# The second chunk's attention outputs summed three products behind the gate, with the decode columns formed apart

## The chip, the cores and the metric

The kernel runs on one core of one Trainium2 chip. The core has a matrix engine (TensorE, PE in the profile, with its weight loads as PEld), three engines for elementwise work (VectorE, DVE; ScalarE, ACT; GpSimd, POOL) and a queue engine (SyncE, SP) that issues most of the DMA transfers; GpSimd issues the others. The metric is device time in microseconds, and a time is the median of the runs. TensorE's granted clock is given as a share of full speed.

## The reference

The kernel computes one inference step of a two-layer decoder of width 2048, with 1024 prompt tokens and 8 decode tokens. Layer A is a pooling mixer. Layer B, where the change lies, is sliding-window attention over keys and values shared from layer A's output, with 32 query heads of 64, a learned sink per head and a gate:

```python
def attn_layer(x, pos, kb, vb, k_pos, q_pos, blocked, w_in, sinks, w_out, g_ln, b_ln):
    z = x @ w_in                                   # 2048 -> queries (2048) and gate (2048)
    q = rope_partial(z[..., :D_ATTN].reshape(B, T, N_HEADS, HEAD_DIM), pos)
    gate = z[..., D_ATTN:]
    ...
    o = attn_core(q, kb, vb, q_pos, k_pos, sinks).reshape(B, T, D_ATTN)
    y = (o * jax.nn.silu(gate)) @ w_out            # 2048 -> 2048
    return layer_norm(ALPHA * x + y, g_ln, b_ln)
```

`o * silu(gate)` is what this text calls the attention outputs. The prompt tokens go through it blocked by the window of 128, the 8 decode tokens against a cache of keys and values.

## The kernel before

Tokens are columns. Chunk 0 holds prompt tokens 0 to 511, chunk 1 the tokens 512 to 1023 and, as its last 8 columns, the decode tokens (520 columns). Features lie on the 128 partitions in 16 tiles. The phases run one after another: `ai`, `ao` (layer A, in and out), `bi` (layer B's keys, values, queries and gate, with the attention mixed in) and `bo` (output projection), each for chunk 0 and chunk 1; in the profile's order of time they end with bi of chunk 0, bi of chunk 1 (called bi1, first product at 1542.9 us), bo of chunk 0 (bo0, from 1990.3) and bo of chunk 1 (bo1, from 2172.8).

**Products.** Most matrix work goes through Strassen's scheme: a block of two by two quarters takes seven products in place of eight. One product is 24 matmuls (`seven`, L641 to L643): eight contraction tiles, each as weight-high by input-high, weight-high by input-low and weight-low by input-high. High is a rounded cast on ScalarE (L474 for weights, L752 for inputs), low the rest, subtracted on VectorE (L489 and L761). The lines L582 to L614 move the products' results out of the accumulators on ScalarE and VectorE (L602 and L607 are VectorE's).

**Sums of inputs.** Four of the seven products of a block use sums of quarters of the input: E and O are two neighbouring feature tiles, a and b the two halves of their columns. `t_ops` (L809 to L812) forms the four sums on VectorE in a fresh slot, GpSimd's queue stores them to a tensor in DRAM (L813; `to` for the attention outputs), and the slot is freed at once. When the phase that needs them comes near, `x_load` reads them back (L742).

**Slots.** Nearly everything lives in 53 slots of 128x1040 floats (`Mem`; `m` in the profile). A request takes the whole slot that has been free for longest, or a half one. A slot that is freed with a store still in flight is marked ten releases younger, so that others go first if there are others. A write to a slot waits for the store that still reads it.

**The order.** Every engine executes the program in its written order (`in_order`). That order is set by counting products: `at(n, f)` puts work n products ahead, after that product's matmuls; `product(n, rank, f)` does so for matmuls. `begin` fetches the weights ahead: up to 7 products loaded, 4 cast and 3 complete, less in bi1 when under four whole slots are free (`ahead`). Side work (`side`, `extra`) advances by a step between products as slots allow: the sums of output weights (`sum_gen`, L422 to L428, tensor `swob`) in bi1, and `t_gen` in bo0.

**Attention.** `attend` spreads one pair of heads (tile t) over about 14 products: scores (L1742), the copy and the mask (L1759, L1763), exponentials (L1778), normalization (L1791), transposes (L1795), copies of the transposed weights (L1804, L1805), value products (L1819), and last `gate`: VectorE multiplies the outputs by the gate (L1828) into half a slot, and GpSimd stores the 512 prompt columns (L1831). In chunk 0 `gate` also runs `t_ops` at every second tile. In chunk 1 it doesn't, since the decode tokens' outputs come from elsewhere (`decode`, whose last step `s9` stores eight tiles by eight columns from `sgd` to the same DRAM tensor, L1966); there both are joined in DRAM, and in bo0, from product 18, `t_gen` reads the pairs of tiles back (L822) and runs `t_ops` on them, one pair every second product.

The scores need the rotated queries: `q_done` and `rope` (L1607, L1714) run on VectorE in program order with everything else there.

Of the kernel before, what the change touches and what calls it, by code (L numbers as in the profile page):

```python
# [9 lines left out]
F32 = mybir.dt.float32  # L10
# [6 lines left out]
P = 128  # L17
D = 2048
NK = D // P
SEQ = 1024  # L20
NDEC = 8
# [3 lines left out]
NH = 32  # L25
# [5 lines left out]
TP = 512  # L31
# [39 lines left out]
)  # L71

LATE = (2, 3)
X_KEEP = 5
X_AGE = 3
SIDE_KEEP = 5
# [105 lines left out]
class Kern:  # L182
    def __init__(self, ctx, tc, io):
        self.tc, self.io = tc, io
        self.nc = tc.nc
        pool = lambda name, **kw: ctx.enter_context(tc.tile_pool(name=name, **kw))
        one = pool("one", bufs=1)
        self.smp = pool("smp", bufs=2)
        dram = pool("dram", bufs=1, space=bass.MemoryType.DRAM)
        self.psd = [pool(f"psd{i}", bufs=1, space=bass.MemoryType.PSUM) for i in range(3)]  # L190
        self.pso = pool("pso", bufs=1, space=bass.MemoryType.PSUM)
        self.four = None
        ctx.callback(self.use_four, None)
        self.prm = one.tile([P, N_PRM], F32, name="prm")
        self.cst = one.tile([P, N_CST], F32, name="cst")
        self.mki = one.tile([P, P], I32, name="mki")
        self.jr = one.tile([P, P], F32R, name="jr")
        self.nsink = one.tile([P, NH], F32, name="nsink")
        self.carry = one.tile([P, NK, NST], F32, name="carry")
        self.kdec = one.tile([P, 2, NDEC], F32, name="kdec")  # L200
        self.qd = [one.tile([P, NDEC, 8], F32, name=f"qd{i}") for i in range(2)]
        self.sgd = [one.tile([P, 8, NDEC], F32, name=f"sgd{i}") for i in range(2)]
        self.mem = Mem(pool("mem", bufs=1), NSLOT)
        self.n = 0
        self.i = self.e = self.lastO = self.turns = self.ring = 0
        self.posts, self.events, self.side = [], {}, []
        self.extra, self.on = None, False
        self.fresh = False
        self.ahead = 7, 4, 3
        dr = lambda n, s: dram.tile(s, F32, tag=n, name=n)  # L210
        self.Td, self.act, self.l_sq, self.l_sh = {}, {}, {}, {}
        for c, (_, T) in enumerate(CHUNKS):
            for n, k in (("x", "ai"), ("g", "ao"), ("h", "bi"), ("o", "bo")):
                if (k, c) in STRASSEN:
                    self.Td[n, c] = dr(f"t{n}{c}", [P, 8, 4, T // 2])
            self.act["x", c] = io[f"x{c}"]
            for n in ("g", "h", "o", "p"):
                self.act[n, c] = dr(f"{n}{c}", [P, NK, T])
        self.gbd = dram.tile([32, 2 * P], F32, tag="gbd", name="gbd")
        self.ws = {  # L220
            n: [dr(f"s{n}{q}", [P, 4, 1024]) for q in range(np_)]
            for n, np_ in (("wia", 16), ("woa", 8), ("wkv", 2), ("wib", 16), ("wob", 8))
        }
# [230 lines left out]
    def sums(self, name, q):  # L454

        self.hurry = name
        while self.summed.get(name, 16) <= q:
            if name != "wob":
                self.side_step()
            elif next(self.extra, 1):  # L460
                self.extra = None
        self.hurry = None
# [263 lines left out]
    def x_load(self):  # L726
        i, g = k = self.xl.pop(0)
        key = self.xkey
        T = CHUNKS[key[1]][1]
        TH = T // 2  # L730
        s = self.mem.full()
        if self.xseven:
            t = s.v(4, TH)
            if i in (0, 4, 5):
                k0, h = {0: (0, 0), 4: (1, 1), 5: (1, 0)}[i]
                src = self.act[key][:, 8 * g + k0 : 8 * g + 8 : 2, h * TH : (h + 1) * TH]
            else:
                src = self.Td[key][:, 4 * g : 4 * g + 4, {1: 0, 2: 1, 3: 2, 6: 3}[i], :]
        else:
            t = s.v(2, T)  # L740
            src = self.act[key][:, 4 * g + i : 4 * g + 4 : 2, :]
        self.nc.sync.dma_start(t, src)  # L742
        self.xraw[k] = s, self.i

    def x_cast(self, k):
        if k not in self.xraw:
            assert k == self.xl[0]
            self.x_load()
        s, _ = self.xraw.pop(k)
        n = 4 * (CHUNKS[self.xkey[1]][1] // 2) if self.xseven else 2 * TP  # L750
        h = self.mem.full()
        self.nc.scalar.copy(h.r[:, :n], s.a[:, :n])  # L752
        self.xhi[k] = s, h, n, self.i

# [536 lines left out]
    def phase_end(self, c, xs, x_in, pre, acc, gc, bc, out):  # L1291
# [14 lines left out]
        X, Y, gx, box = {}, {}, {}, {}  # L1306
        io = self.io
        A2 = slice(0, 2 * P)
        four = self.small(NK * 4, 1)
        f3 = four[:].rearrange("p (k t) -> p k t", k=NK)  # L1310
        b2 = lambda x: x[:, None, :].to_broadcast([P, 2, TH])

        def less(p):
# [414 lines left out]
    def attend(self, c, t, at, s1, s2, late=False):  # L1728
# [96 lines left out]
        def gate():  # L1825
            a = self.ao[c, t] = self.mem.half()
            z, j = self.sg.pop((c, t))
            nc.vector.scalar_tensor_tensor(  # L1828
                a.a[:, :TP], x["o"][:, :TP], 0.5, z.a[:, j * T : j * T + TP], op0=ALU.mult, op1=ALU.mult
            )  # L1830
            nc.gpsimd.dma_start(self.act["o", c][:, t, :TP], a.a[:, :TP])  # L1831
            if c == 1:
                self.ao.pop((c, t)).free(True)
            elif t % 2:
                e = self.ao.pop((c, t - 1))
                self.t_ops(e.a[:, :TP], a.a[:, :TP], self.Td["o", c], t // 2, T // 2)
                e.free(True)
                self.ao.pop((c, t)).free(True)
            if j == 1 or t == 15 or self.sg.get((c, t + 1), (None,))[0] is not z:
                z.free()  # L1840

# [6 lines left out]
        self.at(at + s1 + 1, keep)  # L1848
        self.product(at + s1 + s2, 1, values)
        self.at(at + s1 + s2 + 1, gate)  # L1850

    def gate_done(self, c, t0, s, n):
        nc = self.nc
# [28 lines left out]
    def decode(self, c, pr):  # L1882
# [77 lines left out]
        def s9():  # L1960
            a3 = self.sgd[pr][:]
            nc.vector.scalar_tensor_tensor(
                a3, x["p"][:, :64].rearrange("p (b t) -> p t b", t=8), 0.5, a3,
                op0=ALU.mult, op1=ALU.mult,
            )
            nc.sync.dma_start(self.act["o", c][:, 8 * pr : 8 * pr + 8, TP:], a3)  # L1966
            x["v"].free()
            W.free()

# [111 lines left out]
    def run(self):  # L2081
# [10 lines left out]
        def add(key, gen):  # L2092
            self.needs.append((key, gen))
            self.side.append(gen)

        acc, before = {}, False
        for n, (kind, c, part) in enumerate(PHASES):
# [20 lines left out]
            if n == 0:  # L2118
                pass
            elif (kind, c) == ("ai", 0):  # L2120
                add(("x", 1, False), self.t_gen(("x", 1)))
                self.room = 99
            elif (kind, c) == ("ai", 1):
                add(("g", 0, False), self.t_gen(("g", 0)))
                self.summed["woa"] = 0
                add("woa", self.sum_gen("woa"))
                self.every = 1.7
            elif (kind, c) == ("ao", 0):
                self.every = 2
            elif (kind, c) == ("ao", 1):  # L2130
                gen = self.ln_gen(0, *acc[0], C_GA, C_BA, self.act["h", 0], None)
                self.at(3, lambda gen=gen: add(("h", 0, True), gen))
                self.every = 2
            elif (kind, c) == ("bi", 0) and not self.strassen:
                self.summed["wob"] = 0
                self.extra = self.sum_gen("wob")
                for k in (4, 24):
                    self.at(k, lambda k=k: setattr(self, "on", k == 4))
                add(("h", 1, False), self.ln_gen(1, *acc[1], C_GA, C_BA, self.act["h", 1], self.Td.get(("h", 1))))
                add(("h", 0, False), self.t_gen(("h", 0)))  # L2140

                for k in range(10):
                    self.at(2 * k + 3, lambda: self.side and self.lastO < self.i - 1 and self.side_step())
                self.every = 1.2
            elif (kind, c) == ("bi", 1):
                self.at(8, lambda: setattr(self, "on", True))
                self.every, self.room = 1, 0
            elif (kind, c) == ("bo", 0):
                self.at(23, lambda: setattr(self, "ahead", (7, 4, 3)))
                self.at(18, lambda: add(("o", 1, False), self.t_gen(("o", 1))))  # L2150
                self.at(16, lambda: [s.free() for s in self.kv])
                self.rt.free()
            elif (kind, c) == ("bo", 1):
                gen = self.ln_gen(0, *acc[0], C_GB, C_BB, io["y0"], None)
                self.at(3, lambda gen=gen: add("y", gen))
                self.every = 3
# [154 lines left out]
```

## Time and profile before

| | |
|---|---|
| time before, median of 3 runs (lowest to highest) | 2367.22 us (2366.88 to 2370.61) |
| profiled execution, its own time | 2367.62 us |
| span from the first to the last instruction | 2365.9 us |
| TensorE busy | 2326.4 us, 98% |
| VectorE busy | 1923.5 us, 81% |
| ScalarE busy | 1342.2 us, 57% |
| GpSimd busy | 201.5 us, 9% |
| mean granted TensorE clock | 0.996 |

A busy share is the time in which an engine executes something, over the span. "Idle before, <- releaser" tells which instruction ended the time in which an engine stood idle; a DMA as a releaser is named by what it writes and reads, as in `to<-m`. Tiles are named without their numbers: `m` is any slot, `pD`, `pS` and `pO` are accumulators, `sm` small tiles. L numbers are lines of the kernel before; where the changed kernel's lines differ, the text says so.

### The profile page before, as it was taken

To read this page: it belongs to the slowest core of one execution; us is meant where nothing else is said; L and a number is where in the kernel's file an instruction comes from. 1 tells how busy PE (TensorE), PEld (TensorE's weight loads), DVE (VectorE), ACT (ScalarE), POOL (GpSimd) and SP (SyncE) were. 2 spreads that over 40 slices of the span, in tenths; PEclk is the share of its full clock that TensorE was granted. 3 is DMA by queue.
4 is the path that set the end of the run, shared out by engine and by line. 5 is a ranking of instruction groups with operands and counts; after the bars stand their busy time and mean duration, and the time that the engine had idled before them with its cause. 6 is when DMAs were issued, how large, how long until landed. Compare 5 with 4: busy or idle time off the path is not lost. (4 is left out here: it accounts for less than half of the span.)

```text
span 2365.9 us, 46542 instructions
## 1 busy us (share of the span) xinstructions
PE 2326.4 (98%) x18424; PEld 2219.4 (94%) x18424; DVE 1923.5 (81%) x2385; ACT 1342.2 (57%) x2429; POOL 201.5 (9%) x379
## 2 busy tenths in 40 slices
PE   8999999999999999999999999999999999999997
PEld 6899999999999999998778899999999999999997
DVE  8787998776878878868888888887777768888887
ACT  4444446544536547554554656685666667546556
POOL 0111110001000000000111111100000000000000
PEclk9999999999999999999999999999999999999999
DMA  8678789889889989989888766788787768699785
GB/s 294 215 244 303 274 291 349 308 308 315 286 278 365 331 270 324 334 314 330 282 324 322 258 230 224 238 297 275 232 259 221 222 193 298 227 353 371 259 302 194
DMA packets 252059, 669.18 MB, mean 283 GB/s; under 512 B 25760, under 2 KB 106560, under 8 KB 251840
## 3 DMA queue, kind: packets, MB, share of 16 engines
q1 hardware_dynamic: 206368, 501.14, 64.0%
q0 software_dynamic: 45472, 165.07, 17.9%
q8 instruction: 144, 2.36, 0.4%
q14 instruction: 75, 0.61, 0.1%
HBM read 471.01 MB, written 185.59 MB: 278 GB/s over the span
## 5 line engine op out<-in xcount | busy, mean ns | idle before, releaser
L641 PE MATMUL pD<-m,m 128*128 128x260 f32 (+1 forms) x4752 | 1346.9, 283 | 9.9 <-DVE m L602 3.7
L643 PE MATMUL pD<-m,m 128*128 128x260 f32 (+1 forms) x4752 | 1340.5, 282 | 4.5 <-DVE m L489 4.5
L642 PE MATMUL pD<-m,m 128*128 128x260 f32 (+1 forms) x4752 | 1340.3, 282 | 0.0
L641 PEld LDWEIGHTS pD<-m,m 128*128 128x128 f32 x4752 | 896.0, 189 | 21.0 <-issue 10.2
L643 PEld LDWEIGHTS pD<-m,m 128*128 128x128 f32 x4752 | 896.7, 189 | 6.0 <-DVE m L489 6.0
L642 PEld LDWEIGHTS pD<-m,m 128*128 128x128 f32 x4752 | 896.3, 189 | 0.5
L489 DVE TENSOR_TENSOR m<-m,m 128x1024 fp32r<-128x1024 f32 x674 | 814.1, 1219 | 96.1 <-ACT m L474 58.3
L474 ACT CAST m<-m 128x1024 fp32r<-128x1024 f32 x674 | 701.6, 1048 | 305.2 <-DVE m L332 71.3
L669 PE MATMUL pD<-m,m 128*128 128x512 f32 x448 | 179.7, 401 | 8.0 <-ACT m L752 8.0
L670 PE MATMUL pD<-m,m 128*128 128x512 f32 x448 | 177.2, 396 | 0.5 <-DVE m L761 0.5
L671 PE MATMUL pD<-m,m 128*128 128x512 f32 x448 | 177.2, 396 | 0.0
L761 DVE TENSOR_TENSOR m<-m,m 128x1024 fp32r<-128x1024 f32 (+1 forms) x120 | 146.9, 1225 | 7.2 <-ACT m L752 5.7
L614 ACT COPY m<-pD 128x260 f32<-128x260 f32 (+1 forms) x83 | 31.0, 373 | 188.2 <-PE pD L643 188.1
L752 ACT CAST m<-m 128x1024 fp32r<-128x1024 f32 (+1 forms) x120 | 125.7, 1052 | 14.2 <-PE pD L670 5.2
L669 PEld LDWEIGHTS pD<-m,m 128*128 128x128 f32 x448 | 84.7, 189 | 29.9 <-ACT m L752 8.0
L332 DVE TENSOR_TENSOR m<-m,m 128x1024 f32<-128x1024 f32 x88 | 107.6, 1222 | 5.9 <-DMA m<-in_wia 4.2
L670 PEld LDWEIGHTS pD<-m,m 128*128 128x128 f32 x448 | 84.8, 189 | 20.4 <-DVE m L761 1.6
L671 PEld LDWEIGHTS pD<-m,m 128*128 128x128 f32 x448 | 84.6, 189 | 19.8
L602 DVE TENSOR_TENSOR m<-pD,m 128x260 f32<-128x260 f32 (+1 forms) x86 | 36.4, 424 | 81.9 <-PE pD L643 78.6
L1778 ACT ACTIVATE m<-m,sm 128x128 f32<-128x128 f32 x256 | 99.2, 390 | 0.0
L1071 PE MATMUL pD<-m,m 128*128 128x260 f32 (+1 forms) x528 | 91.5, 323 | 0.0
L607 DVE TENSOR_TENSOR m<-pD,m 128x260 f32<-128x260 f32 (+1 forms) x84 | 35.6, 424 | 64.2 <-PE pD L643 64.0
(243 smaller groups left out, 2167.3 us busy)
## 6 DMA issues: line engine op xcount, KB each, us to landing
m<-in_wia SPq DMA_DIRECT2D x124, 512.0 KB
m<-in_wib SPq DMA_DIRECT2D x120, 512.0 KB
swia<-m POOLq DMA_DIRECT2D x64, 512.0 KB, 4.9
m<-swia SPq DMA_DIRECT2D x64, 512.0 KB
m<-swoa SPq DMA_DIRECT2D x64, 512.0 KB
swib<-m POOLq DMA_DIRECT2D x64, 512.0 KB, 5.3
m<-swib SPq DMA_DIRECT2D x64, 512.0 KB
m<-swob SPq DMA_DIRECT2D x56, 512.0 KB
```

The lines of the kernel that those rows point to most:

```text
L332: self.nc.vector.tensor_add(s[out].a[:, :1024], s[x].a[:, :1024], s[y].a[:, :1024])
L474: self.nc.scalar.copy(hi.r[:, :1024], self.stream[self.cast].src().a[:, :1024])
L489: self.nc.vector.tensor_sub(lo.r[:, :1024], s.src().a[:, :1024], hi.a[:, :1024])
L641: nc.tensor.matmul(ps[:, :TH], wh[:, s], h, start=new and k == 0, stop=False, skip_group_check=on)
L642: nc.tensor.matmul(ps[:, :TH], wh[:, s], l, start=False, stop=False, skip_group_check=on)
L643: nc.tensor.matmul(ps[:, :TH], wl[:, s], h, start=False, stop=k == 7, skip_group_check=on)
L669: nc.tensor.matmul(ps[:], wh[:, s], h, start=par == 0 and k == 0, stop=False)
L670: nc.tensor.matmul(ps[:], wh[:, s], l, start=False, stop=False)
L671: nc.tensor.matmul(ps[:], wl[:, s], h, start=False, stop=par == 1 and k == 7)
L752: self.nc.scalar.copy(h.r[:, :n], s.a[:, :n])
L761: self.nc.vector.tensor_sub(l.r[:, :n], s.a[:, :n], h.a[:, :n])
L1778: nc.scalar.activation(x["s3"][:, i, :], x["s3"][:, i, :], AF.Exp, bias=nm[:, i : i + 1], scale=0.125, accum_out=rs[:, i : i + 1],)
```

## The change

- In chunk 1, `gate` sets the last 8 columns of its half slot to zero on GpSimd, and copies columns 252 to 259 of the tile (the 8 columns of the second half's prompt tokens that stand opposite to the decode tokens) to a small tile `oa`.
- At every second tile `gate` runs `t_ops` on the two half slots over all 520 columns, for chunk 1 not at once but three products later, and frees the two half slots then. For chunk 0 the sums stay where they were.
- `t_gen` for the attention outputs of chunk 1, with its eight loads of 520 KB, is gone from bo0.
- The sums' columns that involve decode tokens are formed apart: `o_dec`, called by `gate` and by `decode`, counts its calls for each half of the tiles; when the eight tiles and the decode result are there, four small VectorE operations on 4x8 columns write them to `otd`, one product later.
- When bo1's inputs are cast (`x_cast`), ScalarE first writes these columns from `otd` over the loaded sums (eight small copies).
- `phase_end` takes its small tile `four` from `oa` in place of a tile of its own.

```diff
+TROW = {1: 0, 2: 1, 3: 2, 6: 3}
...
+        self.oa = one.tile([P, NH // 2, NDEC], F32, name="oa")
+        self.otd = one.tile([P, NK // 2, 4, NDEC], F32, name="otd")
+        self.odn = {}
...
         h = self.mem.full()
+        if self.xkey == ("o", 1) and k[0] in TROW:
+            t = s.v(4, THM)[:, :, THM - NDEC : THM]
+            self.nc.scalar.copy(t, self.otd[:, 4 * k[1] : 4 * k[1] + 4, TROW[k[0]], :])
         self.nc.scalar.copy(h.r[:, :n], s.a[:, :n])
...
-        four = self.small(NK * 4, 1)
-        f3 = four[:].rearrange("p (k t) -> p k t", k=NK)
+        four = self.oa[:].rearrange("p k t -> p (k t)")[:, : NK * 4]
+        f3 = four.rearrange("p (k t) -> p k t", k=NK)
...
             nc.gpsimd.dma_start(self.act["o", c][:, t, :TP], a.a[:, :TP])
             if c == 1:
-                self.ao.pop((c, t)).free(True)
-            elif t % 2:
+                nc.gpsimd.memset(a.a[:, TP:T], 0.0)
+                nc.gpsimd.tensor_copy(self.oa[:, t, :], a.a[:, THM - NDEC : THM])
+                self.o_dec(t // 8)
+            if t % 2:
                 e = self.ao.pop((c, t - 1))
-                self.t_ops(e.a[:, :TP], a.a[:, :TP], self.Td["o", c], t // 2, T // 2)
-                e.free(True)
-                self.ao.pop((c, t)).free(True)
+
+                def sums():
+                    self.t_ops(e.a[:, :T], a.a[:, :T], self.Td["o", c], t // 2, T // 2)
+                    e.free(True)
+                    self.ao.pop((c, t)).free(True)
+
+                if c == 1:
+                    self.at(3, sums)
+                else:
+                    sums()
...
+    def o_dec(self, pr):
+
+        self.odn[pr] = self.odn.get(pr, 0) + 1
+        if self.odn[pr] < 9:
+            return
+
+        def go():
+            nc = self.nc
+            d, o = self.sgd[pr][:], self.oa[:, 8 * pr : 8 * pr + 8, :]
+            Ea, Oa, Eb, Ob = o[:, 0:8:2, :], o[:, 1:8:2, :], d[:, 0:8:2, :], d[:, 1:8:2, :]
+            t = self.otd[:, 4 * pr : 4 * pr + 4]
+            nc.vector.tensor_sub(t[:, :, 1, :], Ea, Eb)
+            nc.vector.tensor_sub(t[:, :, 2, :], Eb, Ob)
+            nc.vector.tensor_add(t[:, :, 0, :], Ob, t[:, :, 1, :])
+            nc.vector.tensor_sub(t[:, :, 3, :], Oa, t[:, :, 0, :])
+
+        self.at(1, go)
...
             nc.sync.dma_start(self.act["o", c][:, 8 * pr : 8 * pr + 8, TP:], a3)
+            self.o_dec(pr)
...
                 self.at(23, lambda: setattr(self, "ahead", (7, 4, 3)))
-                self.at(18, lambda: add(("o", 1, False), self.t_gen(("o", 1))))
                 self.at(16, lambda: [s.free() for s in self.kv])
```

More of the change, by code (lines that the diff above doesn't have):

```diff
@@ L737, in x_load @@
             else:
-                src = self.Td[key][:, 4 * g : 4 * g + 4, {1: 0, 2: 1, 3: 2, 6: 3}[i], :]
+                src = self.Td[key][:, 4 * g : 4 * g + 4, TROW[i], :]
         else:
```

## The prediction

> **What bounds the kernel now.** I read the page first, then the windows and TensorE's own waits by stage, then the time lines around the gates.
>
> ```profile
> PE 2326.4 (98%) x18424; PEld 2219.4 (94%) x18424; DVE 1923.5 (81%) x2385; ACT 1342.2 (57%) x2429; POOL 201.5 (9%) x379
> ```
> TensorE is busy for 98% of the span, so every microsecond by which it is made to wait comes on top, and work taken from another engine is worth only the waits of TensorE that it ends. The next two views show where those are: the windows of a part of the second chunk's query and gate phase (bi1; columns: PE, PEld, DVE, ACT and POOL busy us, granted clock, DMA share, GB/s) and of the stretch of the first chunk's output phase (bo0) that holds the sums today, then TensorE's waits in all of bo0.
>
> ```profile
> 1540.00:1740.00 200.00, 199.66 (x1751) 194.40 (x1751) 156.90 (x204) 132.54 (x287) 12.61 (x20) 1.00 0.80 264
> ...
> 2075.00:2150.00 75.00, 75.00 (x638) 75.00 (x637) 62.95 (x82) 35.79 (x48) 6.39 (x12) 1.00 1.00 359
> ```
> ```profile
> PE pD L643 <- DVE m L489: 3.5, 5, 1.4
> PE pD L641 <- DVE m L602: 1.0, 1, 1.0
> PE pS L1819 <- DVE m L1805: 0.7, 1, 0.7
> PE pD L641 <- ACT pD L582: 0.3, 1, 0.3
> PE pD L629 <- ACT m L614: 0.3, 1, 0.3
> ```
> In bi1 TensorE does not wait though VectorE is 78% busy (156.9 of 200): it runs ahead. In bo0 it waits 5.8 us in all, but none of that lies in 2075 to 2150, where TensorE is busy 75.00 of 75.00.
>
> **The sums that move.** Eight groups of four VectorE operations leave products 26 to 43 of bo0.
>
> ```profile
> L812 DVE TENSOR_TENSOR m<-m,m 128x260 f32<-128x260 f32 x8 | 3.4, 430 | 0.3
> L809 DVE TENSOR_TENSOR m<-m 128x260 f32<-128x260 f32 x8 | 3.4, 424 | 0.0
> ```
> ```profile
> L813 POOL DMA_DIRECT2D to<-m x8: 531/531/533, 2087.5 to 2132.8; - x8
> ```
> The four are alike, 3.4 us for eight, so 13.6 us; they and their stores run from 2085 to 2133, inside the stretch without a wait. The eight loads of 520 KB on SyncE's queue that go with them fed only these sums. Removing all of it is worth 0; the upper bound is the 5.8 us of bo0 (a rival below). The changed program's instruction order places the groups at products 51, 65, 79, 93, 107 and 120 of bi1, and 6 and 19 of bo0: two stay in bo0. In bi1 a group costs VectorE 1.5 us (start to start of its operations) in place of a part of the output weights' sums, which the order shifts later because fewer slots are free, still inside bi1. VectorE's idle 22% covers it: 0, and 1.5 us each if it did not.
>
> **The stores that go with them.** A group's tile is freed as soon as its store is issued. In the changed program only two to five whole slots are free in bi1, and the next request for a slot takes this very one. Its writer must wait until the store has landed:
> ```
> L816..L819 to tile m43, L820 store m43 (DMASW7); next L493 VectorE m43   [waits DMASW7]   product 51
>                    L820 store m20 (DMASW3); next L277 SyncE load m20  [waits DMASW3]   product 65
>                    L820 store m28 (DMASW0); next L478 ScalarE m28     [waits DMASW0]   product 79
>                    L820 store m40 (DMASW6); next L478 ScalarE m40     [waits DMASW6]   product 93
>                    L820 store m40 (DMASW4); next L493 VectorE m40     [waits DMASW4]   product 107
> ```
> (L820, L478 and L493 are L813, L474 and L489 before.) The last three groups' slots are not asked for soon. What a landing takes, and that such a wait exists today, is in the groups of DMA issues (last column: median us to landing), in the answer for the tile `to`, and in ScalarE's waits in bo0:
>
> ```profile
> swob<-m POOLq DMA_DIRECT2D x32, 512.0 KB, 6.0
> ...
> to<-m POOLq DMA_DIRECT2D x8, 520.0 KB, 7.6
> ```
> ```profile
> DMA to landing us min/median/max: 2.9/6.7/9.3
> ```
> ```profile
> ACT m L474 <- DMA to<-m: 7.0, 4, 3.0
> ```
> So landing is between 2.9 and 9.3 us. I take 6.0, since the `swob` stores, of nearly this size, share bi1's lighter DMA load (0.80, against 1.00 where the 7.6 was). The issue starts 0.4 us after the sums (L812 ends near 2087.1, L813 starts at 2087.5), so a slot is blocked for 6.4 us. In bo0 ScalarE waited up to 3.0 us for it without harm; in bi1 the blocked engine has the chain to the next score matmuls behind it. The rows of product 51:
>
> ```profile
> 1716.07 1.23 DVE L489 TENSOR_TENSOR m<-m,m 128x1024 fp32r<-128x1024 f32 x1 [1.04 <-ACT m L1778]
> ...
> 1721.30 1.22 DVE L1805 TENSOR_TENSOR m<-pS,cst 128x1024 f32<-128x1024 f32 x1 [1.11 <-ACT m L1804]
> 1722.44 2.38 DVE L1607 TENSOR_TENSOR m<-m,m 128x1040 f32<-128x1040 f32 x2
> 1724.86 1.24 DVE L1714 TENSOR_TENSOR m<-m,m 128x1040 f32<-128x1040 f32 x1
> ```
> ```profile
> 1727.46 1.78 PE L1742 MATMUL pS<-m,m 64*128 64x256 f32 x14
> ```
> Product 51: the sums end at 1716.6, the store lands at 1723.0. VectorE then has L489, two small ones (0.4), L489, L1805, two L1607 and L1714 in a row: 7.5 us, to 1730.5. Queued behind the wait are thus the next weights' low parts and the rope of the queries; who waits is L1742, which started at 1727.46: **+3.1**. Product 65: a SyncE load some six loads ahead of its use waits: **0** (6.4 at worst, if that lead were gone).
>
> ```profile
> 1819.83 0.29 DVE L1940 TENSOR_SCALAR m<-m,sm 128x128 f32<-128x128 f32 x1
> ```
> ```profile
> 1822.32 1.04 ACT L474 CAST m<-m 128x1024 fp32r<-128x1024 f32 x1
> ...
> 1824.49 1.00 ACT L1804 COPY m<-pS 128x1024 f32<-128x1024 f32 x1
> ```
> ```profile
> 1831.04 2.00 PE L1742 MATMUL pS<-m,m 64*128 64x256 f32 x16
> ```
> Product 79: the sums follow L1940 and end at 1821.5, landing 1827.9. ScalarE is blocked, and behind it stand two casts, the eviction L591, a third cast and L1804 (4.3 us together); then L1805, a small copy, L1607 twice and L1714 on VectorE (5.1): 1837.3, against 1831.04: **+6.3** (of these some 4.1 already at the eviction).
>
> ```profile
> 1867.15 2.36 DVE L489 TENSOR_TENSOR m<-m,m 128x1024 fp32r<-128x1024 f32 x2 [0.26 <-issue]
> ...
> 1916.89 2.36 DVE L489 TENSOR_TENSOR m<-m,m 128x1024 fp32r<-128x1024 f32 x2
> ```
> ```profile
> 1882.36 2.00 PE L1742 MATMUL pS<-m,m 64*128 64x256 f32 x16
> ...
> 1932.48 2.00 PE L1742 MATMUL pS<-m,m 64*128 64x256 f32 x16
> ```
> Product 93: the sums take 1869.4 to 1870.9, landing 1877.3; with the chain of product 79 without the small copy 9.1 us, 1886.4 against 1882.36: **+4.0**. Product 107: 1919.2 to 1920.7, landing 1927.1, 7.5 us as at 51, 1934.6 against 1932.48: **+2.2**. Together **+15.6**. With a landing of L the four are L−2.9, L+0.3, L−2.0 and L−3.8, never below 0.
>
> [...]
>
> **The clock.** A long enough wait of TensorE costs again behind it:
>
> ```profile
> 360.74 0.39 PE L641 MATMUL pD<-m,m 128*128 128x256 f32 x1 [1.94 <-ACT pD L582]
> ```
> ```profile
> PE pD L641 <- ACT m L1778: 2.6, 1, 2.6
> ```
> ```profile
> 360.70:364.80 4.10, 4.06 (x21) 4.06 (x22) 4.07 (x4) 3.22 (x4) 0.53 (x1) 0.59 1.04 371
> 1364.00:1368.30 4.30, 4.30 (x24) 4.30 (x25) 4.26 (x5) 0.85 (x1) 1.06 (x2) 0.61 0.62 250
> ```
> ```profile
> PE pD L641 <- DVE m L602: 1.4, 1, 1.4
> ```
> After waits of 1.94 and 2.6 us the granted clock is 0.59 and 0.61 over some 4 us; after one of 1.4 us (at 2233) no such stretch is seen. In bi1 a matmul takes 199.66 / 1751 = 0.114 us, so the two stretches lost 4.06 − 21 × 0.114 = 1.7 and 4.30 − 24 × 0.114 = 1.6. Of the new waits those of product 79 (4.1) and 93 (2.2 at its eviction) are past 1.9: 2 × 1.6 = **+3.2**; bounds 0 and 4 × 1.6 = 6.4. [...]
>
> **bo0.** VectorE around product 19, where the eighth group and the decode columns' second four operations now stand (ahead of and behind L602):
>
> ```profile
> 2021.97 1.23 DVE L1805 TENSOR_TENSOR m<-pS,cst 128x1024 f32<-128x1024 f32 x1 [2.23 <-ACT m L1804]
> ...
> 2059.11 1.22 DVE L1263 TENSOR_TENSOR m<-m,m 128x1024 f32<-128x1024 f32 x1
> ...
> 2063.65 0.42 DVE L602 TENSOR_TENSOR m<-pD,m 128x256 f32<-128x256 f32 x1
> ...
> 2079.33 3.49 DVE L489 TENSOR_TENSOR m<-m,m 128x1024 fp32r<-128x1024 f32 x3
> ```
> ```profile
> 1822.19 0.17 DVE L1785 TENSOR_TENSOR sm<-sm,sm 128x8 f32<-128x8 f32 x1 [0.32 <-ACT m L1778]
> ```
> VectorE has no gap from 2059 to 2082.8, and TensorE's waits for L489 at products 20 and 22 lie here, so what is added is paid in full: 1.5 for the group, and for four operations on 4x8 columns four times between L1785's 0.17 (8 columns) and L1940's 0.29 above (128 columns), 0.7 to 1.2, 0.9 taken as 32 columns are nearer to the former: **+2.4**; 0 if TensorE's queue of weights were deeper there than the waits say. The seventh group, at product 6, falls ahead of the first row, into 2.23 us of VectorE's idleness: 0, at most 1.5. The first decode four stand in bi1: 0, at most 0.9.
>
> **GpSimd and ScalarE.**
> ```profile
> L1381 POOL COPY sm<-m 128x8 f32<-128x8 f32 x8 | 4.7, 605 | 32.7 <-DVE m L612 29.9 <-DVE m L1263 1.4 <-DMA m<-p 1.4
> ```
> ```profile
> L1864 ACT COPY sgd<-m 128x16 f32<-128x16 f32 x8 | 1.6, 201 | 0.0
> ```
> Sixteen copies of 128x8 at 0.6 us and as many memsets (smaller) are under 20 us of an engine that is 9% busy. They stand behind the store of the gate's output and ahead of later stores; the sums that need them come three products later: 0 (0.6 a gate at most). Eight ScalarE copies at 0.2: one lies ahead of an eviction (L614) that TensorE waits for, **+0.2**; at most 1.6. Taking `four` from another tile costs no instruction: 0.
>
> **Sum:** 15.6 + 3.2 + 2.4 + 0.2 = 21.4. The profiled execution took 2367.62, 0.4 over the median of 2367.22: 2389.0 against its own time, **2388.6** as a median.
>
> **Rivals.**
> - *B, the queues hide it.* Bi1's weights are prepared products ahead, and ScalarE's waits for the same stores in bo0 cost nothing. Then only bo0's 2.6 stays: 2369.8. Against it: L1714 ended at 1726.1, 1.3 us before L1742 at 1727.46, and that is all the lead the rope has.
> - *C, quick landing* at the observed 2.9: 0, 3.2, 0.9 and 0, no fall of the clock past 1.9 save one: 4.1 + 1.6 + 2.6 = 8.3, 2375.5.
> - *D, faster.* If VectorE's 13.6 us out of bo0 let its queue get ahead, TensorE's 5.8 us of waits there go: 2361.4. That decides only if B holds and the eighth group is covered. Against it: the waits lie at products 14 to 22 and 51 to 55, the removed work at 26 to 43, and what VectorE may prepare ahead is limited.
> - *E, late landing.* At the maximum of 9.3 (a POOL queue with a weight store ahead): 6.4 + 9.6 + 7.3 + 5.5 = 28.8, four falls 6.4, bo0 2.6: 37.8, 2405.
>
> **How the numbers follow.** The forecast 0.60 (its own range, landing 4 to 8: 2379 to 2399), B 0.15, C 0.10, D 0.07, E 0.08. A measurement here can tell about 0.2%, 4.7 us, from no change: B is "same", D "faster", the rest "slower" (0.78). The range 2369 to 2401 leaves out D, half of E and the forecast's ends.
>
> **What will show it.** Right: ScalarE's and VectorE's waits list casts (L478, L493) waiting for DMA `to<-m` of 3 to 6 us in bi1; TensorE waits for L1721 or L595 near 1728, 1830, 1885 and 1935, with granted clock under 1 behind two of them; bi1 longer by 15 to 20 us, bo0 by 2 to 3. Wrong: bi1 as long as before (447 us between its first products), or bo0 shorter by its waits. It would be wrong most of all if landings in bi1 differ from 6 us, as each microsecond counts four times.

## The result, and the profile after

The changed kernel takes 2394.49 us (median of 5 runs, 2391.82 to 2396.11) against 2368.41 before (now five runs, the three of above among them): a ratio of 1.0111, 95% interval 1.0099 to 1.0122, so 26 us slower. The forecast was 2388.6 us, slower, in a range of 2369 to 2401. The profiled execution took 2394.49 us with a span of 2392.7, against 2367.62 and 2365.9: 26.8 more in the span. (In the changed kernel L813 is L820, L474 L478, L489 L493, L591 L595, L602 L606, L641 to L643 L645 to L647, L1714 L1721, L1742 L1749, L428 L432.)

From the first product of one phase to that of the next, bi1 takes 475.6 us in place of 447.4 (+28.2), bo0 182.3 in place of 182.5. So the cost is all in bi1. The windows of bi1, of the kernel before and of the changed one (columns: PE, PEld, DVE, ACT, POOL busy us, granted clock, DMA share, GB/s):

```profile
1543.00:1990.30 447.30, 446.45 (x3997) 433.14 (x3996) 330.37 (x431) 298.29 (x689) 23.88 (x38) 1.00 0.76 242
```
```profile
1541.50:2017.10 475.60, 455.44 (x3996) 440.92 (x3997) 339.10 (x458) 298.22 (x688) 31.18 (x70) 0.97 0.71 233
```
TensorE executes the same matmuls, but stands idle for 475.60 − 455.44 = 20.2 us in place of 0.85 (+19.3), and is busy for 9.0 us longer, at a granted clock of 0.97. Both parts are one cause. TensorE's waits in bi1, and the waits of VectorE and of ScalarE for stores of sums:

```profile
PE pD L645 <- ACT m L595: 19.2, 4, 8.0
PE pS L1749 <- DVE m L1721: 0.5, 2, 0.3
PE pD L645 <- ACT pD L586: 0.4, 1, 0.4
```
```profile
ACT m L478 <- DMA to<-m: 7.7, 1, 7.7
```
```profile
DVE m L493 <- DMA to<-m: 12.8, 2, 7.5
```
Four waits of TensorE make up 19.2 us, where before the whole phase had one of 0.85. How one comes about is seen on VectorE and then on ScalarE and TensorE behind the sums of product 51:

```profile
1723.08 1.23 DVE L493 TENSOR_TENSOR m<-m,m 128x1024 fp32r<-128x1024 f32 x1 [7.54 <-DMA to<-m]
```
```profile
1724.34 1.04 ACT L478 CAST m<-m 128x1024 fp32r<-128x1024 f32 x1 [8.70 <-DVE m L493]
1725.29 0.37 ACT L595 COPY m<-pD 128x260 f32<-128x260 f32 x1
```
```profile
1725.71 0.58 PE L645 MATMUL pD<-m,m 128*128 128x260 f32 x1 [4.17 <-ACT m L595]
```
VectorE's L493 writes the slot that the sums have just left, and waits 7.54 us for their store. ScalarE's next cast waits for this L493, the eviction L595 stands behind the cast in ScalarE's order, and TensorE's next product waits for the eviction. Where the cast is itself the one that waits for the store, at product 79, it stands 9.5 us; the landings of all these stores span nearly the same range as before (2.9/6.7/9.3 then):

```profile
1836.03 1.04 ACT L478 CAST m<-m 128x1024 fp32r<-128x1024 f32 x1 [9.49 <-issue]
```
```profile
DMA to landing us min/median/max: 2.9/6.0/9.0
```
(The profile names no releaser there; in the trace the store lands at 1835.96, just ahead of the cast, and the run hold79 below shows that it is the store.) TensorE's four waits are 4.17, 7.96, 5.21 and 1.82 us at products 53, 81, 95 and 109. At each the clock falls; the windows that begin shortly before their ends:

```profile
1725.00:1732.00 7.00, 6.29 (x36) 6.06 (x38) 5.46 (x5) 6.14 (x14) 0.00 (x0) 0.53 0.00 0
1839.00:1848.00 9.00, 8.23 (x68) 7.75 (x70) 7.41 (x10) 7.35 (x15) 0.00 (x0) 0.71 0.16 51
1898.00:1906.00 8.00, 7.21 (x61) 6.78 (x63) 6.55 (x7) 6.92 (x15) 0.00 (x0) 0.73 0.00 2
1952.00:1960.00 8.00, 7.00 (x60) 6.60 (x62) 6.45 (x7) 7.02 (x15) 0.00 (x0) 0.79 0.21 60
```
That DMA is nearly at rest in these windows (0.00 to 0.21, against 0.71 in all of bi1) would fit loads that wait, too, for slots that the stalled engines have yet to leave; no run was made on that.

In bo0 the sum of TensorE's waits is as before, but other ones make it up:

```profile
PE pD L647 <- DVE m L493: 2.9, 4, 1.4
PE pD L645 <- DVE m L606: 1.5, 1, 1.5
PE pD L633 <- ACT m L618: 0.8, 1, 0.8
PE pS L1826 <- DVE m L1812: 0.7, 1, 0.7
```
The wait for L606 at product 20, ahead of which the eighth group and the decode columns now stand, is new (1.5). At products 51 to 55, where 2.6 us were lost before, only 0.8 is left.

### The profile page after: what moved, and what is told of

Its sections match the earlier page's. It is cut to its first block, busy times and chain, and to the rows that moved or that the text cites. A ratio compares the mean times of both kernels' runs of the same rounds, so it can differ in the third digit from the quotient of the medians.

```text
span 2392.7 us, 46615 instructions
## 1 busy us (share of the span) xinstructions
PE 2333.9 (98%) x18424; PEld 2226.5 (93%) x18424; DVE 1925.4 (80%) x2393; ACT 1344.3 (56%) x2437; POOL 207.3 (9%) x411
## 5 line engine op out<-in xcount | busy, mean ns | idle before, releaser
L645 PE MATMUL pD<-m,m 128*128 128x260 f32 (+1 forms) x4752 | 1350.5, 284 | 28.8 <-ACT m L595 19.2
L647 PE MATMUL pD<-m,m 128*128 128x260 f32 (+1 forms) x4752 | 1342.8, 283 | 3.9 <-DVE m L493 3.9
L645 PEld LDWEIGHTS pD<-m,m 128*128 128x128 f32 x4752 | 899.0, 189 | 40.7 <-ACT m L595 20.0
L493 DVE TENSOR_TENSOR m<-m,m 128x1024 fp32r<-128x1024 f32 x674 | 814.6, 1220 | 122.3 <-ACT m L478 71.6
L647 PEld LDWEIGHTS pD<-m,m 128*128 128x128 f32 x4752 | 899.5, 189 | 5.1 <-DVE m L493 5.1
L646 PEld LDWEIGHTS pD<-m,m 128*128 128x128 f32 x4752 | 899.3, 189 | 0.5
L478 ACT CAST m<-m 128x1024 fp32r<-128x1024 f32 x674 | 701.1, 1048 | 329.1 <-DVE m L336 71.8
L673 PEld LDWEIGHTS pD<-m,m 128*128 128x128 f32 x448 | 84.9, 189 | 30.1 <-ACT m L759 8.1
L606 DVE TENSOR_TENSOR m<-pD,m 128x260 f32<-128x260 f32 (+1 forms) x86 | 36.5, 424 | 91.3 <-PE pD L647 91.1
L674 PEld LDWEIGHTS pD<-m,m 128*128 128x128 f32 x448 | 84.9, 190 | 19.9 <-DVE m L768 1.0
L675 PEld LDWEIGHTS pD<-m,m 128*128 128x128 f32 x448 | 84.7, 189 | 19.9
L1078 PEld LDWEIGHTS pD<-m,m 128*128 128x128 f32 x528 | 79.5, 188 | 8.2
```

The lines of the kernel that those rows point to most:

```text
L478: self.nc.scalar.copy(hi.r[:, :1024], self.stream[self.cast].src().a[:, :1024])
L493: self.nc.vector.tensor_sub(lo.r[:, :1024], s.src().a[:, :1024], hi.a[:, :1024])
L645: nc.tensor.matmul(ps[:, :TH], wh[:, s], h, start=new and k == 0, stop=False, skip_group_check=on)
L646: nc.tensor.matmul(ps[:, :TH], wh[:, s], l, start=False, stop=False, skip_group_check=on)
L647: nc.tensor.matmul(ps[:, :TH], wl[:, s], h, start=False, stop=k == 7, skip_group_check=on)
L673: nc.tensor.matmul(ps[:], wh[:, s], h, start=par == 0 and k == 0, stop=False)
```

## The experiments

Theory 1: the cost is the wait for the store of a slot that is taken again at once. Theory 2: it is the work and traffic themselves (VectorE's sums in bi1, the stores on the DMA engines, two half slots held longer). Ratios are to the kernel before, measured beside each group on the same chip; a line of `...` in an edit stands for code left out.

**hold3: the slots of the sums are kept back until their store has landed**

```diff
         nc.gpsimd.dma_start(dst[:, kp], t)
-        s.free(True)
+        if self.ph == "bi1" and self.i > self.i1 + 40:   # i1: the phase's first product
+            self.at(3, s.free)
+        else:
+            s.free(True)
...
+            self.i1 = self.i
```


> The changed kernel, but the slot of each of chunk 1's sums in bi1 is freed three products after its store was issued in place of at once, so the next request gets another slot. Theory 1 (the wait for the store of the reused slot): TensorE's four long waits at products 53, 81, 95 and 109 go (4.2, 8.0, 5.2 and 1.8 us in the changed kernel), with the slow-clock stretches behind them; bi1 is back from 475.6 us to 447 to 449, and the time is 2366 to 2370. Theory 2 (VectorE's sums in bi1, one slot less and the later weight sums cost the time): bi1 stays above 465 us and the time above 2385.

2375.07 us, ratio 1.0035 (1.0022 to 1.0048): some 18 of the 26 us go. All four waits are gone, and the same sums and stores run in bi1. Theory 2 falls as the main cause; theory 1's own number (2366 to 2370) is missed too. TensorE's waits in bi1 and the VectorE row behind the larger one:

```profile
PE pD L647 <- DVE m L493: 3.9, 1, 3.9
PE pS L1752 <- DVE m L1724: 1.5, 1, 1.5
```
```profile
1774.09 2.54 DVE L493 TENSOR_TENSOR m<-m,m 128x1024 fp32r<-128x1024 f32 x2 [6.75 <-DMA swob<-m]
```
With the sums' slot away, the next request took the slot of the output weights' part that VectorE had just summed. Its store to `swob` was issued at 1767.79 and landed 6.1 us later: the same wait on another store. The 1.5 at product 81 is VectorE's: the sums stand ahead of the rope there.

**late8: as hold3, the last group later**

```diff
-                    self.at(3, sums)
+                    self.at(12 if t == 15 else 3, sums)
```


> As hold3, and the last group of sums stands 12 products behind its gate in place of 3, so at product 28 of bo0 and not at 19. Theory: the wait of TensorE at product 20, 1.51 us for L606 in the changed kernel and 0.25 before, falls back, and those that went at products 51 to 55 (2.6 us before, 0.85 in the changed kernel) stay away: 1.2 to 1.8 us less than hold3, bo0 about 180.5 us. Rival (what VectorE saves is used up ahead of product 51 either way): the waits at 51 to 55 come back and bo0 is as in hold3, 182.3.

2374.69 us, ratio 1.0032 (1.0020 to 1.0044). By the medians this is no measurable difference to hold3. The profile shows the step: bo0 takes 180.6 us against 182.4 in hold3, the 1.5 for L606 at product 20 is gone, and 0.6 remains at product 55. Only 0.5 of these 1.8 us are waits, since the wait at product 22 is back (1.3); the rest is a fall of the clock behind product 20 in hold3's profile (granted clock 0.72 in 2076 to 2082). Against the changed kernel, which has no such fall (1.00 in 2093 to 2099), the waits of bo0 are 1.6 us less, as expected. The 3.8 at product 66 stands as in hold3.

**hold79: only the third group's slot is kept back**

```diff
-        s.free(True)
+        if self.ph == "bi1" and kp == 2:
+            self.at(3, s.free)
+        else:
+            s.free(True)
```


> The changed kernel with only the third group's slot (product 79) held for three products. Theory 1: the wait of 8.0 us at product 81 and the slow clock behind it (some 1.9 us) go, the other three stay: about 10 us less than the changed kernel, 2384 to 2386. Theory 2: unchanged within 2 us.

2385.33 us, ratio 1.0076 (1.0062 to 1.0090), 8 us less than the changed kernel by the two ratios, where about 10 were expected. TensorE's waits for L595 are now three:

```profile
PE pD L645 <- ACT m L595: 10.2, 3, 4.8
```
The 8.0 of product 81 is gone with that one slot held back, so the 9.49 that the profile gave no releaser for was the store.

**twice: the store of the first five groups is issued twice**

```diff
         nc.gpsimd.dma_start(dst[:, kp], t)
+        if self.ph == "bi1" and kp < 5:
+            nc.gpsimd.dma_start(dst[:, kp], t)
         s.free(True)
```


> The changed kernel with the store of the first five groups issued twice, the second waiting for the first, so a slot is blocked for two landings. Theory 1: each of the four waits is longer by one more landing (7.0, 9.0, 7.8 and 4.7 us in the changed kernel, 28.6 together): 2415 to 2427, with TensorE's waits in bi1 near 48 us. Theory 2 (stores matter only through the DMA engines' load): under 3 us more, below 2398.

2413.66 us, ratio 1.0195 (1.0182 to 1.0209): some 20 us on top by the two ratios, somewhat less than theory 1 expected.

```profile
PE pD L645 <- ACT m L595: 36.1, 4, 11.1
```
The waits grew by 36.1 − 19.2 = 16.9 us. The second stores landed 4.7, 3.0, 4.8 and 4.3 us after their issue, 16.8 together, not in the 28.6 of the first ones. Product by product, from the first issue to the last landing the slots were blocked 4.0, 2.3, 5.7 and 4.5 us longer than in the changed kernel, and the waits grew by 4.0, 2.5, 5.9 and 4.5: here the waits follow the landings to within 0.2 us, and what was mis-sized in the expectation was the landing.

**holdboth: the weight parts' slots are kept back, too**

The edit against hold3:

```diff
-            self.at(3, s.free)                           # the sums' slot, of hold3
+            self.at(2, s.free)
...
             self.nc.gpsimd.dma_start(self.ws[name][q][:, :, cs], t)
-            s.free(True)
+            if self.ph == "bi1":
+                self.at(2, s.free)
+            else:
+                s.free(True)
```


> The changed kernel; the slot of each of chunk 1's sums and the slot of each part of the output weights' sums in bi1 are freed two products after their stores were issued. In hold3 one wait of this kind was left, at product 66, where the slot of a weight part (store to swob) was taken at once (3.9 us of TensorE and slow clock behind it). Theory 1 (all that the change costs beyond VectorE's 1.5 us at product 81 is the wait for a store of a slot that is taken again at once): the 3.9 us and the slow clock go, bi1 is 447.5 to 450 us, the time 2367 to 2370. Theory 2 (what hold3 kept is VectorE's own work in bi1): the time stays at hold3's 2375.

2369.38 us, ratio 1.0009 (1.0000 to 1.0018): theory 1's range. bi1 takes 448.9 us. What is left there is 1.9 us for the rope at two products:

```profile
PE pS L1755 <- DVE m L1727: 1.9, 2, 1.3
```

**best: as holdboth, with the third group six and the last one twelve products behind the gate**

```diff
-                    self.at(3, sums)
+                    self.at({15: 12, 5: 6}.get(t, 3), sums)
```


> As holdboth, with the third group of sums six products behind its gate (VectorE then forms them after the rope of the next queries, not ahead of it) and the last one twelve products behind. Theory: the 1.5 us before the score matmuls of product 81 and the 1.5 us at product 20 of bo0 go: 2363.5 to 2366.5, 0.05 to 0.15 per cent below the kernel before, bo0 180.6 us. Rival: VectorE's sums come up against something else in bi1; the time is at or above holdboth's.

2368.88 us, ratio 1.0005 (0.9996 to 1.0014), where 2363.5 to 2366.5 was expected. bo0 is 181.1 us and the waits at product 81 and 20 are gone, as the theory had it, but a larger one stands at product 25 (3.2 us), which is ahead of all of chunk 1's sums:

```profile
1629.45 2.39 DVE L1620 TENSOR_TENSOR m<-m,m 128x1040 f32<-128x1040 f32 x2 [5.00 <-DMA m<-m]
```
The rope waits 5.00 us for the transfer that swaps its rows, against 1.37 at this product before. Only the weight parts' slots, kept back from the phase's first product on, differ there.

**lag0: the sums in the gate itself**

```diff
-                if c == 1:
-                    self.at(3, sums)
-                else:
-                    sums()
+                sums()
```


> The changed kernel with chunk 1's sums in the gate itself, no product behind it. No slot of theirs is asked for within about two products of its store. Theory 1 (the immediate reuse of the slot): no wait of TensorE over 1.5 us in bi1, 2368 to 2374; the sums wait for GpSimd's memset behind the issue of the output store (0.6 us), at most 0.7 us of VectorE each. Theory 2 (the sums' work and stores in bi1): above 2385.

2371.65 us, ratio 1.0015 (1.0006 to 1.0024). Same sums, same stores, no slot kept back; only that the slot isn't asked for at once. TensorE waits in bi1 for the eviction L586:

```profile
PE pD L645 <- ACT pD L586: 4.1, 3, 2.5
```
These waits (2.5, 0.9 and 0.7) come from VectorE's queue, in which the sums now stand ahead of the next weights' low parts and of the softmax, not from a store. Behind the 2.5 the clock falls as well (0.69 in 1822.5 to 1828). One was above the 1.5 that was expected; the time is in its range.

**lag6: the sums six products behind the gate**

```diff
-                    self.at(3, sums)
+                    self.at(6, sums)
```


> The changed kernel with chunk 1's sums six products behind the gate. Again no slot of theirs is asked for at once. Theory 1: 2366 to 2374, bi1 447 to 453 us. Theory 2 (holding two half slots longer costs, so six products cost more than three): above 2394.

2372.86 us, ratio 1.0022 (1.0014 to 1.0031). bi1 takes 446.2 us, a microsecond less than before the change: with no reuse the sums there cost nothing. The time is lost in bo0 (189.8), where the group that now falls on product 10 meets the same fate:

```profile
2032.18 1.23 DVE L493 TENSOR_TENSOR m<-m,m 128x1024 fp32r<-128x1024 f32 x1 [5.08 <-DMA to<-m]
```
TensorE waits 4.9 us behind it. The expectation said that no slot would be asked for at once, which held for bi1 alone.

**decalone: the decode columns apart, the sums back in bo0**

```diff
             if c == 1:
                 nc.gpsimd.memset(a.a[:, TP:T], 0.0)
                 nc.gpsimd.tensor_copy(self.oa[:, t, :], a.a[:, THM - NDEC : THM])
                 self.o_dec(t // 8)
-            if t % 2:
+                self.ao.pop((c, t)).free(True)
+            elif t % 2:
...
+                self.at(18, lambda: add(("o", 1, False), self.t_gen(("o", 1))))
```


> One part of the change alone: the kernel before (sums in bo0 from the reloaded outputs) with the decode columns formed apart, GpSimd's sixteen memsets and copies, the eight ScalarE copies and oa for four. Theory (this part is covered, since the changed kernel's bo0 was not longer): the time of the kernel before within 1.5 us, bo0 182 to 183 us. Rival, as the prediction had it: 0.9 at product 19 or 20 of bo0 and 0.2 for a ScalarE copy, bo0 183.5, about 1.1 us more in all.

2368.03 us, ratio 1.0003 (0.9994 to 1.0012): this part is covered. bo0 is 183.1 us, 0.6 more than before; TensorE's waits there:

```profile
PE pD L647 <- DVE m L493: 3.8, 5, 1.4
PE pD L645 <- DVE m L606: 1.0, 1, 1.0
```
The 1.0 for L606 at product 55 and 0.9 for L493 just ahead of it are back, as in the kernel before. So it is the sums' leaving bo0 that takes the waits at 51 to 55 away.

**best2: as best, the weight parts' slots kept back from product 40 on**

```diff
-            if self.ph == "bi1":
+            if self.ph == "bi1" and self.i > self.i1 + 40:
                 self.at(2, s.free)
```


> As best, but the slots of the weight parts are held only from product 40 of bi1 on, as those of the sums are. In best and holdboth a new wait stood at product 25 (TensorE 3.2 and 1.3 us for the rope L1727, and VectorE for a transfer m<-m before it), ahead of all of chunk 1's sums, where only the held weight slots differ. Theory: that wait goes, bi1 is 446 to 447.5 us, bo0 181, the time 2363 to 2366. Rival (the transfer at product 25 comes late by chance of the DMA queues): a wait there of over 1 us stays, the time 2367 to 2369.

2364.82 us against 2367.3 for the kernel before: a ratio of 0.9989 (0.9980 to 0.9998), the only version of the change that is faster than the kernel before. bi1 takes 446.9 us and bo0 181.2. TensorE waits in bi1 for nothing but two evictions, and in bo0 for these:

```profile
PE pD L648 <- ACT pD L589: 0.4, 1, 0.4
PE pD L636 <- ACT m L621: 0.3, 1, 0.3
```
```profile
PE pD L650 <- DVE m L496: 2.8, 4, 1.3
PE pD L636 <- ACT m L621: 0.9, 1, 0.9
PE pS L1832 <- DVE m L1818: 0.7, 1, 0.7
PE pO L650 <- DVE m L496: 0.5, 1, 0.5
```
The wait at product 25 is gone, so it was the slots kept back early, not chance.

## Why the prediction was right

The mechanism is the one the prediction took: the store waits reach TensorE in bi1, four times, at the products it named, and product 65's costs nothing. hold3 and holdboth remove it, twice lengthens it, lag0 and lag6 avoid it. By its steps:

- **Landing, 6.0 us taken.** The four that count landed 7.0, 9.0, 7.8 and 4.7 us after their issue, 7.1 in the mean.
- **The waits, +15.6.** Idle time of TensorE in bi1 grew by 19.3. The prediction's own formulas with the measured landings give 7.0 − 2.9 = 4.1, 9.0 + 0.3 = 9.3, 7.8 − 2.0 = 5.8 and 4.7 − 3.8 = 0.9: 20.1. The size that was off is the landing.
- **The path.** The prediction put most of a wait on the rope and the score matmuls (L1742). The profile has 19.2 us on the eviction L595 and 0.5 on the scores. ScalarE stands in the path even where VectorE is the one that waits for the store, since its next cast waits for that VectorE operation (8.70 us in the row above). As both chains start at the same landing the sum hardly changed.
- **The clock, +3.2.** Four falls, not two: TensorE's busy time in bi1 grew by 9.0 us. The four windows above give (1 − clock) × length = 3.3 + 2.6 + 2.2 + 1.7 = 9.8, of which some 1.0 still lies in the waits themselves. The term was mis-sized by nearly a factor of three, since the waits of 4.17 and 1.82 us came with a fall as well and two of the four falls clearly cost more than the 1.6 of before. One part of this was in the prediction's own numbers: it held waits past 1.9 us to be long enough, but counted only those at an eviction, while its waits of 3.1 and 2.2 us for the score matmuls of products 51 and 107 are past 1.9 too. In the other direction the fall at 361 us, present in the profile of the kernel before, is absent in the changed kernel's (1.5 us less in ai0, 275.3 against 276.8); the change did not cause that: hold3, which holds the whole change, has this fall, as the last section shows.
- **VectorE's sums in bi1, 0 taken.** hold3 has 1.5 us at product 81, where the sums stand ahead of the rope; this is the 1.5 that the prediction named for a group that is not covered. In the changed kernel it is hidden behind the store's wait of 7.96.
- **bo0, +2.4, in fact −0.2.** This term failed. Product 20 did lose most of what it was charged: 1.51 for L606 and 0.57 for L493, where 0.25 stood, +1.8. But the prediction put the removal of the sums at 0, and the waits at products 51 to 55 fell from 2.6 to 0.8. It argued against this in its rival D ("what VectorE may prepare ahead is limited"); VectorE kept enough of the time saved at products 26 to 43 until 51. decalone, with the sums back, has these waits again.
- **GpSimd, ScalarE and the decode columns, +0.2 and 0.9.** decalone: 0.6 us of bo0 together, the time within what can be measured.
- **Rival B** (the queues hide it) is refuted by the 20.2 us; **C** and **E** are the ends of the landing's range, and the landing came between the forecast and E. **D** (faster) holds in part: in best2, once the waits are gone, bo0 is 1.3 us shorter than before and bi1 0.5 by the profiles. The medians differ by 2.5; where the rest comes from is open.

The sum of 21.4 is 5.4 short of the profiled 26.8, and that it is not further off is partly luck: the waits were too low by 3.7 and the clock by 5.8, while bo0 with ScalarE's copy was too high by 2.8 and the fall in ai0 that stayed away took 1.5. Of the signs that the prediction named, the casts and low parts that wait for `to<-m` came as told, but their waits were 5.2 to 9.5 us and not 3 to 6, the clock fell at four of TensorE's waits and not at two, bi1 grew by 28.2 and not by 15 to 20, and bo0 did not grow.

## What to carry to other kernels

A buffer that is freed when its store is issued isn't free. With two to five whole slots free the allocator gave it here to the very next request, and VectorE or ScalarE, which execute in the written order, stood still for 5.2 to 9.5 us until the store had landed, with all that was queued behind them; look at which request follows each release, and keep the buffer back for two or three steps (hold3 and holdboth, which end the 19.2 us of TensorE's waits for L595), or move the release to where no request follows (lag0). Keeping more back than needed moved the wait elsewhere (3.2 us at product 25 in best, none there in best2), so hold only what is asked for at once.

## What the runs showed of the hardware that was not expected

In these profiles no one length of a wait decides whether the clock falls. The same wait of 1.94 us at 361 us is in the profile of the kernel before and in that of the changed one; in the first some sixteen matmuls behind it run at half speed (0.21 us from start to start in place of 0.12), in the second none. hold3 has a fall there like the kernel before. The changed kernel and hold3, in the same window:

```profile
360.00:366.00 6.00, 4.84 (x41) 4.85 (x42) 5.96 (x6) 5.87 (x9) 0.53 (x1) 1.00 1.04 360
```
```profile
360.00:366.00 6.00, 5.12 (x30) 5.13 (x31) 5.97 (x6) 4.53 (x8) 0.53 (x1) 0.72 1.00 358
```
The wait of 2.6 us near 1364 is followed by a fall in the kernel before and in the changed one (granted clock 0.61 and 0.73 in 1364 to 1368.3). The one of 1.5 us at product 20 of bo0 is followed by a fall in hold3 (0.72 in 2076 to 2082), and by none in the changed kernel (1.00 in 2093 to 2099); that of 3.2 us at product 25 in best has none either (1.00 in 1633 to 1637), while the changed kernel's four in bi1, of 1.82 to 7.96 us, each have one.

What separates these cases in the kernel before and the changed one is in their traces' record of the granted clock. Every fall inside the span lasts 3.41 us or a multiple of it (3.41 and 3.41 in the kernel before; 3.41 near 1364 and 6.83, 10.24, 6.83 and 3.41 at the four waits of bi1 in the changed one, and 3.41 at its end). The falls of one trace start whole multiples of 3.41 us apart: 294 in the kernel before, and in the changed one 106, 138, 156, 173 and 298 behind its first. So each of the two traces can be cut into steps of 3.41 us. With TensorE's idle time summed in each full-speed step between 30 and 2330 us, the steps with 1.94 and 2.45 us in the kernel before and with 2.57, 3.22, 2.21, 2.04 and 1.82 in the changed one were followed by a step at half speed; none of the others was, and the most that one of them had is 1.73. The wait at 361 us lies in one step in the kernel before (busy 1.47 of 3.41, so 1.94 idle) and across two in the changed one (1.73 idle in the second); each with the step that follows it:

```profile
358.01:361.42 3.41, 1.47 (x12) 1.27 (x11) 3.41 (x4) 3.41 (x5) 0.00 (x0) 1.00 0.96 296
361.42:364.83 3.41, 3.41 (x18) 3.41 (x17) 3.38 (x4) 2.50 (x4) 0.53 (x1) 0.50 1.05 386
```
```profile
359.42:362.84 3.42, 1.69 (x14) 1.69 (x15) 3.38 (x4) 3.42 (x5) 0.00 (x0) 1.00 1.01 344
362.84:366.25 3.41, 3.41 (x32) 3.41 (x31) 3.41 (x4) 3.28 (x6) 0.53 (x1) 1.00 1.07 367
```
The 1.82 us of product 109 lie in one step. So, by an estimate from the steps of these two profiles alone, whether waits of 1.82 and 1.94 us cost more than themselves depended on where they fell against the steps.
